# Four raw weight tiles, ten heads kept on chip and a sum load on another queue in a one-core transformer layer

## The chip, the cores and the metric

One core of a Trainium2 chip runs the whole layer. The metric is device time in microseconds, from launch to end. Most executions of one kernel agree within 0.3%.

## The reference, cut to what matters

DEPTH is 1, so the layer is one forgetting-attention (FoX) block and one squared-ReLU MLP, all in float32, for 512 positions of width 2048, 16 heads of 128 and an inner MLP width of 8192.

```python
h = rmsnorm(x, norm_g[0, 0])
q, k, v, f = split(h @ w_in)                      # 3 x 2048 columns and 16 gates
cum = cumsum(log_sigmoid(f + b_f))
logits = q @ k.T * 128**-0.5 + cum_i - cum_j      # causal, per head
h = concat_heads(softmax(logits) @ v) @ w_out
x = x + rmsnorm(h, norm_g[0, 1])
h = square(relu(rmsnorm(x, norm_g[0, 2]) @ w1)) @ w2
x = x + rmsnorm(h, norm_g[0, 3])
```

## The kernel before, in words

**Split products.** Every float32 operand is cut into a high part (a cast by ScalarE, ACT) and a low part (a subtraction by VectorE, DVE), and each product is three matmuls: high by high, high by low, low by high (`mm3`, lines 94 to 96, and `mm3b`, lines 451 to 453). So a weight block on its way to TensorE (PE) passes three stations: a load issued on the queue of SyncE (SP) into a raw tile, an ACT cast, and a DVE subtraction (`load_split`, lines 87 to 89, and `split7`, lines 429 and 430).

**Sevens.** 30 of the 32 blocks of the MLP (a block is 256 of its 8192 inner columns) use a seven-product scheme in place of eight products: a raw tile gets four loaded quarters (512 KB), DVE makes three sums of them (lines 443 to 445), and the seven slots are split at once (`load_seven`). A raw tile has eight slots, and the split reads slots 1 to 7. Three raw tiles take turns (`spool`, `bufs=3`). The split seven goes to one of three places (`tplaces`); one such weight unit feeds 42 matmuls. The other two blocks of the first product are "plain": `plain(hf, p)` runs eight input blocks for the first half of the positions and again for the second half, and loads and splits its weights both times.

**Order of the work.**
1. Projections and attention, head by head, up to about 655 us. `values` copies the output of head h to a tile (tag `o32`, four buffers) and stores it in DRAM (`od`, line 352). The output projection loads all 16 heads back (`split_o`, lines 390 to 393).
2. The output projection: four column blocks c, each with four PSUM banks `py`, all from the pool `psum_acc`; after each block `evac_y` multiplies and squares them (lines 498, 499). Then residual, norm and transposition (`turn`, in the banks of `psum_att`), then `plain` into the banks `ph` of `psum_acc`.
3. The first MLP product: `evac` of the two plain blocks (relu, square, sums: lines 683, 667, 671 to 674), then 30 blocks n of four weight units g each. The squared results go to DRAM (`hd`).
4. The second MLP product: five chunks of six blocks. A chunk is four column pieces cp, each of six weight units k (8 banks in turn), and its sums are added into DRAM by accumulating stores (`md`, line 805) on the queue of GpSimd (POOL). Its left operand is fetched by `want(n)`: a load of 896 KB on POOL's queue into an `h7` tile (`hpool`, two buffers, line 657) and the same split, into a ring of eight places.
5. In the last chunk `gather(cp - 1)` reads the finished sums of the piece before back (`m`, two loads of 896 KB on SP's queue, line 752) into two tiles of `spool`, after the weight unit k = 3 of piece cp, and DVE combines them (lines 755 to 761). `last_w` loads the weights of the two plain blocks into tiles of `spool` too (lines 726 to 729).
6. The tail: `gather(3)`, the products of the plain blocks (`pz`), the last norm, and the output.

Each engine and each queue runs its instructions in the order of the program. A planner sets that order when the kernel is built, from the order of the code, the readiness of operands and free buffers; an instruction that waits holds up all that stand behind it on the same engine or queue.

Of the kernel before, what the change touches and what calls it, by code (L numbers as in the profile page):

```python
# [15 lines left out]
P = 128  # L16
S = 512
# [15 lines left out]
CHUNK = 6  # L33
WARM = 9
# [5 lines left out]
def fox_layer(ctx, tc, xT, x, wq, wk, wv, wf, wo, w1p, w1s, w2s, w2p, gcol, grow, bf, out):  # L40
# [124 lines left out]
    with ExitStack() as att:  # L165
# [106 lines left out]
        ap_ = att.enter_context(tc.tile_pool(name="ap_", bufs=1))  # L272
        def proj(h):
# [25 lines left out]
        def attention(h, res, vs, v32):  # L299
# [44 lines left out]
            def values():  # L344
# [4 lines left out]
                nc.tensor.matmul(ps[:, (TT - 1) * P:], v32[:, c], pts[TT - 1], start=False, stop=True)  # L349
                o = ap_.tile([P, S], F32, tag="o32", name=f"o32_{h}", bufs=4)  # L350
# [72 lines left out]

    AOF = [1, 6, 0, 4, 3, 5, 2]

# [9 lines left out]

    def load_seven(src, name):
# [10 lines left out]
        return split7(raw[:, 1:8], tplaces[tplace[0] % len(tplaces)])  # L447
# [28 lines left out]
    with ExitStack() as trs:  # L476
# [47 lines left out]
        def turn(hf, p):  # L524

            ps = psum_att(f"xT_{hf}_{p}")
# [52 lines left out]
        py = [psum_acc(f"py_{NC - 1}_{t}") for t in range(TT)]  # L579
# [20 lines left out]
        ph = [psum_acc(f"ph_{f}") for f in range(4)]  # L600

        def plain(hf, p):
            w = load_split(w1p[p], f"a{hf}_{p}")
            cols = slice(256 * hf, 256 * (hf + 1))
            for kh in range(2):
# [5 lines left out]
                for f in range(4):  # L611
                    a = [zz[:, kh * 512 + f * P:kh * 512 + (f + 1) * P] for zz in w]
                    mm3(ph[f][:, cols], a, b, p == 0 and kh == 0, p == 7 and kh == 1)
# [12 lines left out]
        for p in range(3):  # L626
            x4[p] = turn(1, p)
            if p < 2:
                m4[p] = mix(p, x4[p])
        for p in range(8):  # L630
            plain(1, p)
            split_mix(p, m4[p])
            if p + 2 < 8:
                m4[p + 2] = mix(p + 2, x4[p + 2])
            if p + 3 < 8:
                x4[p + 3] = turn(1, p + 3)
# [273 lines left out]
```

## Time and profile before

| | us |
|---|---|
| three runs | 2239.34, 2237.58, 2233.78 |
| median | 2237.58 |
| the profiled execution | 2236.39 |
| its span, first to last instruction | 2234.6 |
| PE busy in the span | 2133.5 (95%) |
| DVE, ACT, POOL busy | 1501.1, 958.5, 258.2 |
| PE's granted clock, mean of the span | 0.983 |

Busy PE time is counted from the start to the modelled end of each matmul, and matmuls overlap, so a full PE row says only that it never had to wait. A granted clock of 1.00 is the level of 2.4 GHz and 0.50 that of 1.2 GHz; a mean between them tells how much of a stretch was at each.

### The profile page before, as it was taken

Reading aid. Unit: us, or ns where it says so; the run is one execution under the profiler, and the core shown is the slowest. Engines: PE = TensorE matmul, PEld = TensorE weight load, DVE = VectorE, ACT = ScalarE, POOL = GpSimd, SP = SyncE. Lnnn points to the kernel's source line nnn. Section 1 sums busy time; section 2 is a strip of 40 time slices with the busy share of each in tenths; the row PEclk is TensorE's granted clock in tenths of the full one; section 3 lists DMA queues with packets and bytes.
Section 4 is the critical chain, followed back from the end, with each engine's and each line's share of the span. In section 5 each row is a group of like instructions: output and inputs, shape, how many; then the busy total and the mean of one; then the engine's idle time right before and its main releaser. Section 6 shows DMA issues by size and latency. Waiting matters only on the chain.

```text
span 2234.6 us, 34858 instructions
## 1 busy us (share of the span) xinstructions
PE 2133.5 (95%) x14450; PEld 1979.9 (89%) x14450; DVE 1501.1 (67%) x2007; ACT 958.5 (43%) x1141; POOL 258.2 (12%) x342
## 2 busy tenths in 40 slices
PE   8999999999989998999999999999999999999785
PEld 6788888888867878999999999999999999998774
DVE  9553453544542368888888888888777767676656
ACT  4433332333332356444444444445554545453341
POOL 8000000000010000000000000001122122211113
PEclk9999999999999999999999999999999999999998
DMA  5333333333352364544445444456586878677567
GB/s 176 105 104 94 101 98 99 100 94 104 91 192 89 118 228 145 194 161 163 159 144 166 163 159 143 162 189 231 182 239 164 241 171 239 169 200 187 148 180 225
DMA packets 112351, 352.94 MB, mean 158 GB/s; under 512 B 12080, under 2 KB 23472, under 8 KB 107712
## 3 DMA queue, kind: packets, MB, share of 16 engines
q1 hardware_dynamic: 82656, 246.58, 34.3%
q0 software_dynamic: 29392, 104.12, 17.5%
q8 instruction: 113, 1.85, 0.3%
q14 instruction: 46, 0.38, 0.0%
q10 hardware_dynamic: 144, 0.02, 0.0%
HBM read 268.85 MB, written 81.82 MB: 157 GB/s over the span
## 4 chain that ended last, share of the span: by engine, by line
PE 64%; issue 20%; DVE 7%; POOL 4%; DMA 3%; ACT 1%; SPq 0%; POOLq 0%; DVEq 0%; ACTq 0%
PE ps L453 9%; PE ps L452 9%; PE ps L451 9%; POOL md L805 4%; PE pq L96 3%; PE pk L96 3%; PE pk L94 3%; PE pq L95 3%; PE pk L95 3%; PE pq L94 3%; PE py L94 2%; PE py L95 2%; PE py L96 2%; PE pv L95 2%; PE pv L96 2%
## 5 line engine op out<-in xcount | busy, mean ns | idle before, releaser
L452 PE MATMUL po<-opr 128*128 128x256 f32 x1204 | 343.7, 287 | 24.0 <-DVE opr L430 24.0
L451 PE MATMUL po<-opr 128*128 128x256 f32 x1204 | 337.7, 285 | 6.5 <-ACT opr L429 4.3
L453 PE MATMUL po<-opr 128*128 128x256 f32 x1204 | 341.9, 285 | 0.0
L451 PE MATMUL ps<-opr 128*128 128x256 f32 x1120 | 318.2, 284 | 6.6 <-ACT opr L429 6.6
L452 PE MATMUL ps<-opr 128*128 128x256 f32 x1120 | 318.0, 284 | 0.0
L453 PE MATMUL ps<-opr 128*128 128x256 f32 x1120 | 317.4, 284 | 0.2 <-DVE opr L430 0.2
L452 PEld LDWEIGHTS po<-opr 128*128 128x128 f32 x1204 | 234.0, 194 | 26.9 <-DVE opr L430 26.7
L451 PEld LDWEIGHTS po<-opr 128*128 128x128 f32 x1204 | 230.9, 194 | 8.4 <-ACT opr L429 5.7
L453 PEld LDWEIGHTS po<-opr 128*128 128x128 f32 x1204 | 233.9, 194 | 0.0
L451 PEld LDWEIGHTS ps<-opr 128*128 128x128 f32 x1120 | 216.2, 193 | 6.8 <-ACT opr L429 6.8
L452 PEld LDWEIGHTS ps<-opr 128*128 128x128 f32 x1120 | 216.1, 193 | 0.0
L453 PEld LDWEIGHTS ps<-opr 128*128 128x128 f32 x1120 | 215.7, 193 | 0.5 <-DVE opr L430 0.5
L429 ACT CAST opr<-seven_b 128x1792 fp32r<-128x1792 f32 x86 | 145.2, 1689 | 144.2 <-DVE seven_b L445 68.6
L430 DVE TENSOR_TENSOR opr<-seven_a,opr 128x1792 fp32r<-128x1792 f32 x80 | 161.9, 2024 | 51.5 <-ACT opr L429 50.2
L429 ACT CAST opr<-seven_a 128x1792 fp32r<-128x1792 f32 x80 | 134.7, 1684 | 142.4 <-PE ps L452 131.4
L430 DVE TENSOR_TENSOR opr<-seven_b,opr 128x1792 fp32r<-128x1792 f32 x86 | 173.5, 2020 | 18.5 <-ACT opr L429 18.5
L443 DVE TENSOR_TENSOR seven_b<-seven_b 128x512 f32<-128x512 f32 x120 | 82.7, 689 | 125.7 <-DMA seven_b<-in_w2s 124.9
L451 PE MATMUL ps<-opr,w 128*128 128x256 f32 x560 | 158.5, 283 | 0.0
L452 PE MATMUL ps<-opr,w 128*128 128x256 f32 x560 | 158.5, 283 | 0.0
L453 PE MATMUL ps<-opr,w 128*128 128x256 f32 x560 | 158.5, 283 | 0.0
L452 PE MATMUL po<-w,opr 128*128 128x256 f32 x476 | 136.8, 288 | 9.4 <-DVE w L430 9.4
L805 POOL DMA_DIRECT2D md<-st x112 | 100.2, 1483 | 355.2 <-ACT st L801 354.4
(231 smaller groups left out, 5275.7 us busy)
## 6 DMA issues: line engine op xcount, KB each, us to landing
seven_a<-in_w1s SPq DMA_DIRECT2D x120, 512.0 KB, 3.6
seven_b<-in_w2s SPq DMA_DIRECT2D x120, 512.0 KB, 4.6
md<-st POOLq DMA_DIRECT2D x140, 256.0 KB, 8.1
hd<-ev POOLq DMA_DIRECT2D x30, 1024.0 KB, 4.4
h<-hd POOLq DMA_DIRECT2D x30, 896.0 KB, 5.6
raw_o<-in_wo SPq DMA_DIRECT2D x40, 512.0 KB, 3.5
raw_q<-in_wq SPq DMA_DIRECT2D x32, 512.0 KB, 3.7
raw_k<-in_wk SPq DMA_DIRECT2D x32, 512.0 KB, 3.7
```

Source lines behind the costliest of these rows:

```text
L94: nc.tensor.matmul(o, a[0], b[0], start=start, stop=False)
L95: nc.tensor.matmul(o, a[0], b[1], start=False, stop=False)
L96: nc.tensor.matmul(o, a[1], b[0], start=False, stop=stop)
L429: nc.scalar.copy(hi, z)
L430: nc.vector.tensor_tensor(out=lo, in0=z, in1=f32(hi), op=ALU.subtract)
L443: nc.vector.tensor_tensor(out=raw[:, 4:6], in0=raw[:, 1:3], in1=raw[:, 0:1].to_broadcast([P, 2, 256]), op=ALU.add)
L451: nc.tensor.matmul(o, a[0], b[0], start=start, stop=False, skip_group_check=True)
L452: nc.tensor.matmul(o, a[0], b[1], start=False, stop=False, skip_group_check=True)
L453: nc.tensor.matmul(o, a[1], b[0], start=False, stop=stop, skip_group_check=True)
L805: nc.gpsimd.dma_start(md[cp, :, j], st, accum_op=ALU.add)
```

## The change

- `spool` has four raw tiles of seven slots; the third and fourth sum overwrite slot 0 and fill slot 6, and `BOF` tells the matmuls where each of the seven now is. `hpool` has one `h7` tile in place of two.
- `gather` loads `m` on POOL's queue, after k = 5 in place of k = 3.
- The outputs of heads 0 to 9 stay in tiles of their own; heads 10 to 15 go through DRAM as before.
- The second half of the plain blocks runs in the order 5, 6, 7, 4, 0, 1, 2, 3 and uses the split weights of 5, 6 and 7 that the first half left; the first seven block (n = 2) takes its units in the order 3, 2, 0, 1, and the evacuation of the two plain blocks comes after the second and third of them.
- Column blocks of the output projection alternate between the two PSUM pools, and `ph`, `turn` and the banks of the first product swap pools to fit.

```diff
@@ values / split_o
+                if h < KEEP:
+                    o32[h] = ap_.tile([P, S], F32, tag=f"o32_{h}", name=f"o32_{h}")
+                    nc.scalar.copy(o32[h], ps)
+                    return
...
-            o = ap_.tile([P, S], F32, tag="o32", name=f"o_{h}", bufs=4)
-            nc.sync.dma_start(o, od[h])
+            o = o32.get(h)
+            if o is None:
+                o = ap_.tile([P, S], F32, tag="o32", name=f"o_{h}", bufs=4)
+                nc.sync.dma_start(o, od[h])
@@ load_seven
-        raw = spool.tile([P, 8, 256], F32, tag="seven", name=f"seven_{name}")
+        raw = seven(f"seven_{name}")
         nc.sync.dma_start(raw[:, 0:4], src)
...
-        nc.vector.tensor_tensor(out=raw[:, 6], in0=raw[:, 4], in1=raw[:, 2], op=ALU.add)
-        nc.vector.tensor_tensor(out=raw[:, 7], in0=raw[:, 3], in1=raw[:, 6], op=ALU.add)
+        nc.vector.tensor_tensor(out=raw[:, 0], in0=raw[:, 4], in1=raw[:, 2], op=ALU.add)
+        nc.vector.tensor_tensor(out=raw[:, 6], in0=raw[:, 3], in1=raw[:, 0], op=ALU.add)
@@ turn, output projection, plain
-            ps = psum_att(f"xT_{hf}_{p}")
+            ps = psum_acc(f"xT_{hf}_{p}")
...
-            py = [psum_acc(f"py_{c}_{t}") for t in range(TT)]
+            py = [(psum_att if c % 2 else psum_acc)(f"py_{c}_{t}") for t in range(TT)]
...
-        ph = [psum_acc(f"ph_{f}") for f in range(4)]
+        ph = [psum_att(f"ph_{f}") for f in range(4)]
...
-            w = load_split(w1p[p], f"a{hf}_{p}")
+            order = LATE if hf else range(8)
+            if hf == 0 or p < 5:
+                w[p] = load_split(w1p[p], f"a{hf}_{p}")
@@ pools
-    spool = second.enter_context(tc.tile_pool(name="spool", bufs=3, reuse_waits="tile"))
+    spool = second.enter_context(tc.tile_pool(name="spool", bufs=4, reuse_waits="tile"))
...
-    hpool = hs_.enter_context(tc.tile_pool(name="hpool", bufs=2, reuse_waits="tile", side="right"))
+    hpool = hs_.enter_context(tc.tile_pool(name="hpool", bufs=1, reuse_waits="tile", side="right"))
@@ first MLP product
-        for n in range(2):
+        def evac_plain(n):
...
+            order = [3, 2, 0, 1] if n == 2 else range(4)
+            for g in order:
...
+                if n == 2 and g in order[1:3]:
+                    evac_plain(order.index(g) - 1)
@@ gather
-            nc.sync.dma_start(m, md[cp, :, :, t * 256:(t + 1) * 256])
+            nc.gpsimd.dma_start(m, md[cp, :, :, t * 256:(t + 1) * 256])
...
-                        if cp > 0 and k == 3:
+                        if cp > 0 and k == 5:
```

## Rows read from the trace of the kernel before

**Rows 1.** Page: busy time of PE, and its share of 40 equal slices in tenths.
```profile
PE 2133.5 (95%) x14450; PEld 1979.9 (89%) x14450; DVE 1501.1 (67%) x2007; ACT 958.5 (43%) x1141; POOL 258.2 (12%) x342
...
PE   8999999999989998999999999999999999999785
```

**Rows 2.** Busy time by stretch: length, PE, PEld, DVE, ACT, POOL, clock, DMA, GB/s.
```profile
655.00:682.97 27.97, 18.01 (x72) 14.04 (x71) 8.58 (x12) 6.88 (x11) 0.71 (x2) 0.88 0.47 151
...
865.00:897.20 32.20, 19.99 (x160) 19.00 (x159) 29.76 (x48) 19.50 (x30) 0.55 (x1) 0.93 0.27 94
897.20:1503.00 605.80, 605.58 (x5025) 605.28 (x5026) 516.36 (x687) 276.00 (x216) 18.09 (x34) 1.00 0.48 163
1503.00:1538.00 35.00, 30.02 (x242) 29.00 (x242) 31.14 (x32) 20.82 (x16) 3.70 (x7) 1.00 0.76 255
1538.00:1630.00 92.00, 92.00 (x769) 92.00 (x768) 70.22 (x78) 47.72 (x43) 13.38 (x25) 1.00 0.62 203
...
1752.00:1880.00 128.00, 123.47 (x1013) 122.87 (x1012) 93.51 (x103) 64.06 (x59) 28.30 (x35) 0.99 0.77 201
1880.00:2007.00 127.00, 122.27 (x1004) 121.86 (x1004) 92.27 (x102) 63.92 (x58) 27.71 (x34) 0.99 0.77 197
...
2037.10:2078.40 41.30, 34.21 (x263) 33.40 (x262) 23.66 (x38) 14.07 (x14) 6.19 (x7) 0.92 0.67 166
2078.40:2122.10 43.70, 33.46 (x254) 32.78 (x254) 25.30 (x38) 13.66 (x15) 6.21 (x7) 0.88 0.64 157
2122.10:2172.50 50.40, 41.27 (x288) 38.12 (x287) 32.14 (x42) 21.35 (x25) 6.21 (x7) 0.97 0.68 188
```

**Rows 3.** Waits of PE, whole run: who for whom, us in total, times, longest.
```profile
PE py L94 <- ACT opr L392: 8.4, 3, 6.2
PE ps L451 <- ACT opr L429: 6.6, 1, 6.6
PE ph L96 <- DVE opr L89: 5.5, 3, 2.7
...
PE py L94 <- ACT py L499: 3.7, 1, 3.7
```

**Rows 4.** Two short stretches right after PE waits, columns as in rows 2.
```profile
663.74:667.20 3.46, 3.46 (x8) 2.74 (x9) 1.72 (x3) 1.52 (x3) 0.00 (x0) 0.50 0.57 197
...
897.20:902.70 5.50, 5.28 (x23) 4.98 (x24) 5.47 (x6) 4.30 (x7) 0.54 (x1) 0.50 0.72 251
```

**Rows 5.** DVE by line and shape, 865 to 897.2 us: busy, mean ns.
```profile
L89 DVE TENSOR_TENSOR opr<-raw_a,opr 128x1024 fp32r<-128x1024 f32 x5 | 6.1, 1219 | 0.0
```

**Rows 6.** ACT by line and shape, 865 to 905 us.
```profile
L683 ACT ACTIVATE ev<-ph 128x256 f32<-128x256 f32 x8 | 2.4, 387 | 0.7 <-DMA hd<-ev 0.7
L667 ACT ACTIVATE ev<-ev 128x1024 f32<-128x1024 f32 x2 | 2.1, 1056 | 0.1
```

**Rows 7.** Timeline of POOL's queue, 1480 to 1545 us: start, us, what.
```profile
1494.25 0.54 POOL L657 DMA_DIRECT2D h<-hd  x1 [0.56 <-DVE opr L430]
...
1510.65 0.53 POOL L657 DMA_DIRECT2D h<-hd  x1 [5.90 <-DVE opr L430]
```

**Rows 8.** Timeline of ACT, 1488 to 1530 us.
```profile
1515.39 1.69 ACT L429 CAST opr<-h 128x1792 fp32r<-128x1792 f32 x1 [3.55 <-DMA h<-hd]
```

**Rows 9.** Page: costliest groups, the two halves of a seven's split.
```profile
L429 ACT CAST opr<-seven_b 128x1792 fp32r<-128x1792 f32 x86 | 145.2, 1689 | 144.2 <-DVE seven_b L445 68.6
...
L430 DVE TENSOR_TENSOR opr<-seven_b,opr 128x1792 fp32r<-128x1792 f32 x86 | 173.5, 2020 | 18.5 <-ACT opr L429 18.5
```

**Rows 10.** Page: DMA issues, count, KB each, median us to landing.
```profile
h<-hd POOLq DMA_DIRECT2D x30, 896.0 KB, 5.6
```

**Rows 11.** Timeline of DVE, 1757 to 1764 us.
```profile
1759.89 0.69 DVE L443 TENSOR_TENSOR seven_b<-seven_b 128x512 f32<-128x512 f32 x1 [2.27 <-DMA seven_b<-in_w2s]
```

**Rows 12.** Waits of SP's queue, 2037 to 2176 us.
```profile
SPq L752 <- DMA md<-st: 29.4, 3, 13.9
```

**Rows 13.** DMA view, 2037 to 2078.4 us, 40 equal slices.
```profile
GB/s 0 111 334 194 168 204 178 218 186 204 198 198 95 8 0 28 224 331 371 304 351 172 0 103 317 158 214 281 146 245 71 0 0 0 8 162 340 139 289 75
```

**Rows 14.** Timeline of DVE in the tail.
```profile
2194.73 1.39 DVE L755 TENSOR_TENSOR m<-m 128x256 f32<-128x256 f32 x1 [9.75 <-DMA m<-md]
```

More of the change, by code (lines that the diff above doesn't have):

```diff
@@ L33 @@
 CHUNK = 6
+KEEP = 10
 WARM = 9
@@ L424, in fox_layer @@
     AOF = [1, 6, 0, 4, 3, 5, 2]
+    BOF = [1, 2, 3, 4, 5, 0, 6]
     def split7(z, parts):
@@ L578, in fox_layer @@
         load_g1(NC - 1)
-        py = [psum_acc(f"py_{NC - 1}_{t}") for t in range(TT)]
+        py = [psum_att(f"py_{NC - 1}_{t}") for t in range(TT)]
         for hf in range(2):
@@ L611, in plain @@
                 for f in range(4):
-                    a = [zz[:, kh * 512 + f * P:kh * 512 + (f + 1) * P] for zz in w]
-                    mm3(ph[f][:, cols], a, b, p == 0 and kh == 0, p == 7 and kh == 1)
+                    a = [zz[:, kh * 512 + f * P:kh * 512 + (f + 1) * P] for zz in w[p]]
+                    mm3(ph[f][:, cols], a, b, p == order[0] and kh == 0, p == order[-1] and kh == 1)
         for p in range(8):
@@ L625, in fox_layer @@
         x4, m4 = {}, {}
[L626 to L636, printed above, removed]
+        for i in range(3):
+            x4[i] = turn(1, LATE[i])
+            if i < 2:
+                m4[i] = mix(LATE[i], x4[i])
+        for i in range(8):
+            plain(1, LATE[i])
+            split_mix(LATE[i], m4[i])
+            if i + 2 < 8:
+                m4[i + 2] = mix(LATE[i + 2], x4[i + 2])
+            if i + 3 < 8:
+                x4[i + 3] = turn(1, LATE[i + 3])
     first.close()
     second = ctx.enter_context(ExitStack())
-    spool = second.enter_context(tc.tile_pool(name="spool", bufs=3, reuse_waits="tile"))
+    spool = second.enter_context(tc.tile_pool(name="spool", bufs=4, reuse_waits="tile"))
     hs_ = ctx.enter_context(ExitStack())
     wthird = hs_.enter_context(tc.tile_pool(name="wthird", bufs=1, reuse_waits="tile", side="right"))
-    hpool = hs_.enter_context(tc.tile_pool(name="hpool", bufs=2, reuse_waits="tile", side="right"))
+    hpool = hs_.enter_context(tc.tile_pool(name="hpool", bufs=1, reuse_waits="tile", side="right"))
     w3 = wthird.tile([P, 2 * SLOT + 24], F32R, name="w3")
@@ L704, in fox_layer @@
         for n in range(2, NPAIR):
-            b = [(psum_acc if n % 2 else psum_att)(f"ps_{n}_{i}") for i in range(4)]
-            for g in range(4):
+            b = [(psum_att if n % 2 else psum_acc)(f"ps_{n}_{i}") for i in range(4)]
+            order = [3, 2, 0, 1] if n == 2 else range(4)
+            for g in order:
                 w = load_seven(w1s[n - 2, g], f"a{n}_{g}")
@@ L710, in fox_layer @@
                     for kk in range(2):
-                        p = 2 * g + kk
-                        mm3b(b[bi][:, part * 256:(part + 1) * 256], [zz[:, j, kk * P:(kk + 1) * P] for zz in w], xop(p, AOF[j]),
-                             p == 0 and FIRST[bi] == j, p == 7)
+                        mm3b(b[bi][:, part * 256:(part + 1) * 256], [zz[:, BOF[j], kk * P:(kk + 1) * P] for zz in w], xop(2 * g + kk, AOF[j]),
+                             g == order[0] and kk == 0 and FIRST[bi] == j, g == order[-1] and kk == 1)
+                if n == 2 and g in order[1:3]:
+                    evac_plain(order.index(g) - 1)
                 if n == NPAIR - 1 and g > 0:
@@ L719, in fox_layer @@
     NCHUNK = NSTR // CHUNK
-    bank[0] = 4
+    bank[0] = 0
     wlast, hlast = {}, {}
     def last_w(i):
-        raw = spool.tile([P, 8, 256], F32, tag="seven", name=f"raw_z{i}").rearrange("p n c -> p (n c)")[:, 0:1024]
+        raw = seven(f"raw_z{i}").rearrange("p n c -> p (n c)")[:, 0:1024]
         nc.sync.dma_start(raw, w2p[i // 2, i % 2])
```

11 lines of the change are left out of this document (8 added, 3 removed).

## The prediction

> **What bounds the kernel now.** I read the page first: PE is busy for 2133.5 of 2234.6 us, and its slices are full except near two fifths of the span, and in the last three [rows 1]. So nothing that other engines do in the full slices can help; only the holes can. The second view is the busy time by stretch. From 897.2 to 1503 us PE lacks 0.2 us: the first MLP product cannot gain. Between 1538 and 1630 us PE never waits either, and there 769 matmuls take 92.00 us, 0.1196 us each; a weight unit of 42 is 5.02 us and a piece of six units 30.1 us. Those are the yardsticks. Against them stand the holes: 10.0 us idle from 655 to 682.97, 12.2 from 865 to 897.2, 5.0 from 1503 to 1538, 4.5 and 4.7 in two middle chunks, and the pieces cp = 1, 2, 3 of the last chunk, which take 41.3, 43.7 and 50.4 us where 30.1 would do [rows 2]. Of cp = 3, 36 of the 288 matmuls are 512 wide pz products (288 less 6 x 42); at twice 0.1196 us they explain 8.6 us, so the three pieces lose 11.2 + 13.6 + 11.7 = 36.5 us. The third view, PE's waits, names who is late in the first two holes [rows 3]. A clock cost comes on top: just after such waits the granted clock stands at 0.50, the 1.2 GHz level, after PE had idled [rows 4], and work done there takes double. The waits of SP's queue and the DMA view tell what the last chunk stands for: in three gathers SP waits 29.4 us for the accumulating stores to land before it can issue the load of m [rows 12], and in that time the DMA engines fall to 0 to 95 GB/s with weight loads queued behind [rows 13].
>
> **The change part by part.** Negative is a gain.
>
> *Ten heads kept.* PE waits 8.4 us in three waits for the split of a reloaded head, the longest 6.2 us [rows 3]. Ten of 16 stores and reloads go; the six left have ten heads' worth of PE work to hide behind, if the planner moves loads 10 to 12 ahead. Head 15 must still be stored and reloaded, and one store on SP's queue may still stand ahead of loads 11 to 14; then the 6.2 us stay. With the half clock after it, 3.46 us of which half is lost [rows 4], the part is worth 8.4 + 1.7 = 10.1 at most and 2.2 at least (the two short waits). I take 9.3, near the upper end, because four tiles are free for loads 10 to 12 long before.
>
> *Banks in turn.* The wait for `py` squares, 3.7 us once [rows 3], goes: block 1 starts in the other pool, whose banks the attention has left. The later switches show no wait in that list, so they give nothing. -3.7. Swapping `ph` and `turn` only keeps the parity; 0, and if a bank is late there the cost is that of this row.
>
> *Plain blocks kept split, other order.* Three loads and splits go, 3 x 1.22 us of DVE [rows 5], in a stretch where DVE is busy 29.8 of 32.2 us and PE waits 5.5 us for just this split [rows 2, 3]. That takes off 3.7 and leaves about 1.8. Then the hole of 6.6 us before the first seven: ahead of its ACT split stand four relus and a square, 4 x 0.39 + 1.06 = 2.6 us [rows 6], and DVE's share behind them. With the evacuation moved two units later, what remains is the split itself, 1.69 us of ACT [rows 9] and a handover, say 2.2; so 4.4 go. Units 3 and 2 first need blocks 6, 7, 4 and 5 alone, which are mixed first, so the rest of the mixing is covered by 10 us of PE. The half clock from 897.2 to 902.7 cost 2.7 us [rows 4]; I let half of it go, as a shorter hole remains. 3.7 + 4.4 + 1.4 = 9.5; bounds 4 and 14.9 (5.5 + 6.6 + 2.8, all of it). -9.5. Moving the evacuation costs PE nothing while DVE has its spare sixth (516.4 of 605.8 us busy [rows 2]); if that cover fails, it is the 2.6 us again.
>
> *Four raw tiles.* In the middle chunks the PE waits come from a late weight load, as at 1759.89, where DVE itself waits 2.27 us for it [rows 11]: with three tiles the next load is issued only when a split frees one. A fourth puts each load one unit, 5.02 us, earlier, over twice that wait. I count the idle 4.5 + 4.7 us of both chunks as gone: -9.2; bounds 0 and 12 (with the clock at 0.99). The sum in slot 0 in place of slot 6 costs the same DVE work: 0.
>
> *One h7 tile.* This pays for the fourth raw tile, and is the one cost. At the start of the second product six splits of h are wanted one unit apart. With one tile each load waits for the split before: issue to ACT start 4.74 us (1510.65 to 1515.39 [rows 7, 8]), 1.69 of ACT, 2.02 of DVE [rows 9], 0.3 to the next issue: 8.75 us a turn. Now the second is already in its tile at the start. Then its load cannot go before 1494.25 [rows 7], and the sixth is split at 1494.25 + 5 x 8.75 = 1538. PE starts unit 5 at 1538 - 5.02 = 1533 in the trace: 5 us late. With the median landing of 5.6 us [rows 10] and 1 us of queueing at DVE, a turn is 10.6 and the lateness 14. I take +8, as some of the 5 us that PE waits there now [rows 2] falls together with it. At the later chunk starts four turns of 9 us fit the seven to eight units that the ring gives them: 0, bound +8 each (a rival).
>
> *Gather on POOL's queue, two units later.* SP never waits for the stores; weights flow on. POOL has nothing else in the last chunk once the two last h loads are in, so its wait holds nobody until the next stores of sums, a unit later. At k = 5 the stores have had 25 us; the longest wait was 13.9 us [rows 12], so m is there when DVE comes. Two of four tiles are held for some ten us, leaving two for weights. Not all 36.5 us return: the DMA share in these pieces was 0.67, 0.64 and 0.68 of 41.3, 43.7 and 50.4 us [rows 2], 27.7, 28.0 and 34.3 us of transfers, against 30.1 + 30.1 + 38.7 us of PE. cp = 1 and 2 would run the engines over 90% full. I take 32 + 33 + 43.4 = 108.4 in place of 135.4: -27; bounds 12 (only SP's part of cp = 1 and 2) and 36.5. *Against it speaks a rule.* The Trainium skill (DMA: Bandwidth & Descriptors, "Issuing engines are not separate DMA queues") says that DMAs of all queues share the same 16 engines, and that issuing from several saves only the sequencer's time to start them. By that rule alone this part would be near nothing and the time that of the second rival; the idle slices in rows 13 show that here the engines stood without work, which the rule does not speak of.
>
> *The tail.* DVE waits 9.75 us for m, until 2194.73 [rows 14]; the load still waits for the same stores. The reload of x now goes ahead of it and may take bandwidth from the stores: 0, bounds -4 and +8.
>
> **The sum.** 2234.6 - 9.3 - 3.7 - 9.5 - 9.2 + 8 - 27 = 2183.9 us of span. The profiled execution lies 1.8 us above its span (2236.39), and 1.2 us below the median of the runs shown: 2183.9 + 1.8 + 1.2 = 2186.9, so 2187.
>
> **The rivals.**
> 1. *The single h7 tile bites at all five chunk starts.* For it: its split is in order on ACT and DVE, so a late h load holds the weight splits behind it. Against: four turns have 35 us there. 8 us at four more starts, and the middle gain gone: 2187 + 32 + 9 = 2228 at worst, 2214 with two thirds of it.
> 2. *The last chunk stays bound by transfers.* For it: engines over 90% full, eight weight loads more in cp = 3. Only the issue of six loads is saved, some 0.54 us each as POOL's loads take [rows 7]: 3.2 in place of 27: 2211. (The rule of the skill named above gives this.)
> 3. *Slower: POOL's queue stands.* Where an h load waits up to 9 us for its only tile, stores of sums stand behind it, their staging tiles fill, ACT stops at the next copy and with it every split. It decides from 51 us, the whole net gain: six such stops. Twenty pieces offer places, but PE works ahead by two units, 10 us, and covers most: 2245.
> 4. *Everything returns.* No cost at the second product (its present 5 us gone too), all clock losses back: 13.8 + 14.9 + 5 + 12 + 36.5 = 82.2 us: 2155.
> 5. *The reload stall stays,* as the head-15 store stands ahead: 2187 + 7.1 = 2194; inside the range.
>
> **How the numbers follow.** Forecast with its neighbour 5: 0.62, by itself 2172 to 2202. Rival 1: 0.12, rival 2: 0.13, rival 3: 0.06, rival 4: 0.07. The range goes from 2160, which takes in part of rival 4, to 2219, with rival 2 and most of rival 1; outside are 0.04 below and 0.06 + 0.05 above. Faster or slower counts from 0.3%, 6.7 us, which is about what a measurement of this kernel tells from no change. All but rival 3 and the far end of rival 1 are faster: 0.90; same 0.04, slower 0.06.
>
> **What would show it.** In the profile after: no PE wait for L392 and for the squares of py beyond 2 us; a hole of about 2 us at the first seven; SP's queue without a wait for md; pieces of 32 to 33 us in the last chunk and some 43 for the last; a longer stretch for the first piece of the second product, with PE waiting for the split of h. I am wrong if PE waits for splits of h at every chunk, if the last pieces still take over 40 us, or if ACT's copies of po wait for stores through POOL.

## The result and the profile after

The changed kernel takes 2213.11 us (median; 2210.34 to 2215.27) against 2235.68 us for the kernel before: ratio 0.990, 95% interval 0.988 to 0.992. That is faster, by 22.6 us and not by the 50 that I forecast; it lies inside the range. The profiled execution has a span of 2210.4 us, 24.2 less than before. Lines moved: `mm3` is now L95 to L97, `split7` L440 and L441, the seven's sums L457 to L459, `mm3b` L465 to L467, the evacuation L702, L686 and L690 to L692, the load of m L773.

The page: busy time of PE and its 40 slices. The slices answer to [rows 1]: both early holes stay, a new dip stands at the start of the second product (slice 28, 1492 to 1547 us), and the last three are shallower in sum.

```profile
PE 2130.7 (96%) x14450; PEld 1979.9 (90%) x14450; DVE 1498.8 (68%) x2004; ACT 953.0 (43%) x1138; POOL 267.9 (12%) x350
...
PE   8999999999989998999999999998999999999896
```

Busy time by stretch, columns as in [rows 2]: the end of the plain blocks, the first piece of the second product, its three middle chunks, and the four pieces of the last chunk.

```profile
855.00:887.00 32.00, 20.85 (x166) 19.85 (x165) 29.57 (x46) 19.12 (x29) 0.55 (x1) 0.93 0.32 115
...
1494.00:1535.60 41.60, 34.17 (x249) 32.95 (x248) 34.49 (x39) 18.50 (x12) 3.19 (x6) 0.92 0.60 194
1626.60:1749.50 122.90, 121.43 (x1010) 121.03 (x1009) 93.89 (x103) 63.41 (x60) 25.69 (x34) 1.00 0.75 208
1749.50:1875.60 126.10, 123.27 (x1022) 122.46 (x1020) 93.81 (x103) 63.39 (x60) 28.11 (x34) 1.00 0.78 203
1875.60:2003.20 127.60, 122.09 (x996) 120.98 (x995) 93.83 (x103) 63.54 (x60) 28.22 (x34) 0.99 0.77 201
2003.20:2035.90 32.70, 29.86 (x233) 29.26 (x232) 24.74 (x28) 15.17 (x16) 7.87 (x10) 0.95 0.77 201
2035.90:2069.70 33.80, 31.93 (x264) 31.52 (x264) 23.04 (x36) 14.05 (x14) 8.20 (x9) 1.00 0.74 193
2069.70:2107.40 37.70, 32.87 (x255) 32.46 (x253) 24.74 (x38) 13.53 (x14) 8.19 (x9) 0.91 0.72 181
2107.40:2148.10 40.70, 36.37 (x275) 34.77 (x274) 27.34 (x33) 19.01 (x20) 8.18 (x9) 0.96 0.82 229
```

Set against the kernel before by the start of the first instruction of each stage (a piece is counted from its first copy of sums to the next piece's), the span divides so:

| stage | before | after | difference | forecast |
|---|---|---|---|---|
| start to the first `py` product | 622.7 | 618.2 | -4.6 | 0 |
| output projection, to the first `ph` | 207.8 | 202.5 | -5.3 | -13.0 (heads, banks) |
| plain blocks, to the first seven | 66.7 | 66.0 | -0.7 | -9.5 |
| first product | 607.7 | 607.9 | +0.2 | 0 |
| second product, first chunk | 126.0 | 132.0 | +6.0 | +8 |
| its three middle chunks | 378.1 | 376.4 | -1.7 | -9.2 |
| last chunk | 163.4 | 145.0 | -18.4 | -27 |
| from the last piece's copies to the end | 62.1 | 62.3 | +0.2 | 0 |

The first two rows have to be read together. Of the first difference, 1.0 us is the load prologue; the rest is the mark itself, which moved. Before the change, eleven matmuls of the last head's scores (`s`) and a wait of 0.99 us stand ahead of the first `py` product; after it, those eleven run behind the first 24 of `py`. PE of the kernel before, from the first of them to the first `py`:

```profile
619.24 0.39 PE L313 MATMUL s<-k,q 128*128 128x128 f32 x2
...
622.73 0.50 PE L94 MATMUL py<-opr 128*128 128x512 f32 x1 [0.99 <-ACT opr L392]
```

So from the start to the first `ph` product the change gained 9.8 us, 8.9 without the prologue, where heads and banks were to give 13.0. The last chunk holds 12 `pz` products in place of 36, yet the tail that takes up the other 24 is no longer for them: m of the last gather ends it either way.

Waits of PE over the whole run, columns as in [rows 3]. The wait for the squares of `py`, 3.7 us, is gone. The hole before the first seven is still 6.6 us, the reloads still cost 6.5.

```profile
PE po L466 <- DVE opr L441: 18.4, 14, 4.6
PE po L465 <- ACT opr L440: 7.2, 5, 2.7
PE ps L465 <- ACT opr L440: 6.6, 1, 6.6
PE py L95 <- ACT opr L401: 6.5, 2, 5.3
PE ph L97 <- DVE opr L90: 4.5, 4, 1.6
```

### The profile page after: what moved, and what is told of

Read it like the earlier page. It is cut to its first block, busy times and chain, and to the rows that moved or that the text cites. A ratio compares the mean times of both kernels' runs of the same rounds, so it can differ in the third digit from the quotient of the medians.

```text
span 2210.4 us, 34770 instructions
## 1 busy us (share of the span) xinstructions
PE 2130.7 (96%) x14450; PEld 1979.9 (90%) x14450; DVE 1498.8 (68%) x2004; ACT 953.0 (43%) x1138; POOL 267.9 (12%) x350
## 3 DMA queue, kind: packets, MB, share of 16 engines
q1 hardware_dynamic: 72048, 232.42, 32.7%
## 5 line engine op out<-in xcount | busy, mean ns | idle before, releaser
L466 PE MATMUL po<-opr 128*128 128x256 f32 x1204 | 344.7, 287 | 18.5 <-DVE opr L441 18.4
L465 PE MATMUL po<-opr 128*128 128x256 f32 x1204 | 341.1, 286 | 6.2 <-ACT opr L440 6.0
L467 PE MATMUL po<-opr 128*128 128x256 f32 x1204 | 340.4, 285 | 1.1 <-DVE opr L441 1.1
L465 PE MATMUL ps<-opr 128*128 128x256 f32 x1120 | 318.3, 284 | 6.6 <-ACT opr L440 6.6
L467 PE MATMUL ps<-opr 128*128 128x256 f32 x1120 | 317.5, 284 | 0.2 <-DVE opr L441 0.2
L465 PEld LDWEIGHTS po<-opr 128*128 128x128 f32 x1204 | 232.4, 194 | 7.8 <-ACT opr L440 7.0
L467 PEld LDWEIGHTS po<-opr 128*128 128x128 f32 x1204 | 232.6, 194 | 1.5 <-DVE opr L441 1.3
L465 PEld LDWEIGHTS ps<-opr 128*128 128x128 f32 x1120 | 216.2, 193 | 6.8 <-ACT opr L440 6.8
L467 PEld LDWEIGHTS ps<-opr 128*128 128x128 f32 x1120 | 215.8, 193 | 0.5 <-DVE opr L441 0.5
L441 DVE TENSOR_TENSOR opr<-seven_a,opr 128x1792 fp32r<-128x1792 f32 x80 | 161.9, 2024 | 51.5 <-ACT opr L440 50.2
L440 ACT CAST opr<-seven_b 128x1792 fp32r<-128x1792 f32 x86 | 145.1, 1693 | 115.5 <-PE po L467 88.2
L440 ACT CAST opr<-seven_a 128x1792 fp32r<-128x1792 f32 x80 | 134.8, 1685 | 139.0 <-PE ps L466 133.4
L441 DVE TENSOR_TENSOR opr<-seven_b,opr 128x1792 fp32r<-128x1792 f32 x86 | 173.7, 2020 | 19.8 <-ACT opr L440 19.6
L457 DVE TENSOR_TENSOR seven_b<-seven_b 128x512 f32<-128x512 f32 x120 | 82.6, 688 | 125.5 <-DMA seven_b<-in_w2s 125.1
L465 PE MATMUL ps<-opr,w 128*128 128x256 f32 x560 | 158.5, 283 | 0.0
L467 PE MATMUL ps<-opr,w 128*128 128x256 f32 x560 | 158.5, 283 | 0.0
L465 PE MATMUL po<-w,opr 128*128 128x256 f32 x476 | 136.3, 286 | 3.5 <-ACT w L440 2.3
L466 PE MATMUL po<-w,opr 128*128 128x256 f32 x476 | 136.2, 286 | 1.8 <-DVE w L441 1.8
```

Source lines behind the costliest of these rows:

```text
L440: nc.scalar.copy(hi, z)
L441: nc.vector.tensor_tensor(out=lo, in0=z, in1=f32(hi), op=ALU.subtract)
L465: nc.tensor.matmul(o, a[0], b[0], start=start, stop=False, skip_group_check=True)
L466: nc.tensor.matmul(o, a[0], b[1], start=False, stop=False, skip_group_check=True)
L467: nc.tensor.matmul(o, a[1], b[0], start=False, stop=stop, skip_group_check=True)
```

## The experiments

An effect is read from the stage that an edit touches. Ratios are to the kernel before, run beside each; its medians there lay between 2235.5 and 2239.9 us, 4.4 apart, so medians decide only what is larger. All edits are to the changed kernel unless the text says the kernel before.

### The reloaded heads

SP's queue in the changed kernel, timeline from 645 us: start, us, what. The store of head 15 (`od`, L359) waits for that head, and the reloads behind it (L399) are issued only at 651.4 and later. Rival 5 of the prediction.

```profile
645.99 0.43 SPq L399 DMA_DIRECT2D o<-od  x1
651.07 0.33 SPq L359 DMA_DIRECT2D od<-o  x1
651.44 0.94 SPq L399 DMA_DIRECT2D o<-od  x2
652.48 0.40 SPq L88 DMA_DIRECT2D raw_o<-in_wo  x1
654.87 1.10 SPq L399 DMA_DIRECT2D o<-od  x2
```

**e1**, other ten heads:

```diff
-                if h < KEEP:
+                if h >= H - KEEP:
```

> The last ten heads are kept on chip instead of the first ten, so no head that goes through DRAM is stored late. Theory (the store of head 15 stands on SP's queue ahead of the reloads of heads 11 to 14, as the trace of the changed kernel shows): the waits of PE for the split of a reloaded head, 1.19 and 5.33 us, fall to 1.5 us together at most and the half clock that follows them (657.3, 6.8 us) goes with them; the span falls by 5 to 9 us, to 2201 to 2205. Rival (the reloads are late because SP's queue is full of weight loads, or because DMA is busy there): a wait of 4 us or more for a split of a head stays and the span is within 3 us of 2210.

2204.98 us, ratio 0.986 (0.984 to 0.988), span 2201.8. PE has no wait for L401 left, nor the half clock near 657; from the first `py` product to the first `ph` 192.3 us in place of 202.5, -10.2. The theory holds: the number of heads kept was right, the choice of heads was not. From the start to the first `ph` that makes 19.0 us against the kernel before, without the prologue, more than the 13.8 that the prediction allowed for heads and banks together: 12.1 are their waits, and most of the rest goes with the half clock, which stood for 17.0 us of this part before (at 660.5, 684.3 and 814.1) and for 3.4 here, where the prediction took 1.7.

### The hole before the first seven

ACT in the changed kernel, timeline: the evacuation (L702, L686) stands before the first split (L440) as it did before the change, though the code has it later. But ACT then idles 3 us for DVE's last sum (L459), ahead of which DVE ran its own share of the evacuation (L690 to L692, 1.5 us): the relus on ACT were not what came last.

```profile
879.68 1.20 ACT L702 ACTIVATE ev<-ph 128x256 f32<-128x256 f32 x4
880.92 1.06 ACT L686 ACTIVATE ev<-ev 128x1024 f32<-128x1024 f32 x1
884.96 1.69 ACT L440 CAST opr<-seven_a 128x1792 fp32r<-128x1792 f32 x1 [2.99 <-DVE seven_a L459]
```

**e4**, the order forced:

```diff
+        split[0] = nc.scalar.copy(hi, z)                  # in split7
+        split[1] = nc.vector.tensor_tensor(out=lo, ...)
...
-                    evac_plain(order.index(g) - 1)
+                    with tc.issue_after(split[0].ins), tc.issue_after(split[1].ins):
+                        evac_plain(order.index(g) - 1)
```

> The evacuation of the two plain pairs is forced behind the split of the seven that stands ahead of it in the code, on ACT and on DVE; nothing else is changed. Theory (the hole of 6.62 us before the first seven is the relus and the square on ACT, and DVE's share of the evacuation, which were issued ahead of the first split although the code has them later): the hole falls to 2 to 3 us and the span by 4 to 7 us, to 2203 to 2206. Rival (DVE's backlog of mixing sets the start): the hole stays above 5 us and the span within 2 us of 2210, or the work moved behind the split makes PE wait at the second or third seven by as much.

2212.54 us, ratio 0.990 (0.988 to 0.992), span 2206.1. The hole falls from 6.62 to 4.29 us and no further, so neither expectation is met whole; the stage gains 2.3, which the medians cannot tell. ACT and DVE of this run show what is left: the split still waits, now 2.9 us, and DVE reaches the sums (L458) only when the last mixed block is split (L579), which ran behind the half of the mixing that ACT holds.

```profile
882.09 1.69 ACT L440 CAST opr<-seven_a 128x1792 fp32r<-128x1792 f32 x1 [2.86 <-DVE seven_a L460]
```

```profile
879.27 1.22 DVE L579 TENSOR_TENSOR opr<-m,opr 128x1024 fp32r<-128x1024 f32 x1 [1.28 <-ACT opr L578]
880.41 0.68 DVE L458 TENSOR_TENSOR seven_a<-seven_a 128x512 f32<-128x512 f32 x1
```

Sums ahead of the mixing were not tried.

### The last chunk: queue, place or tiles

**e3**, the other queue at the new place; **f1**, the old place with the new queue; **f2**, the kernel before with the new place alone:

```diff
-            nc.gpsimd.dma_start(m, md[cp, ...])           # e3
+            nc.sync.dma_start(m, md[cp, ...])
...
-                        if cp > 0 and k == 5:             # f1; f2 is the reverse, in the kernel before
+                        if cp > 0 and k == 3:
```

> The loads of m are back on SP's queue, at the same place (two units later than in the kernel before). Theory (SP stood for the stores): the last chunk grows from 145 us to 153 or more, as SP again waits some 10 us in each of three gathers, two units later than before; span 2218 to 2226. Rival (the last chunk is bound by raw tiles held by m, or by transfers, whatever queue issues the load, as the Trainium skill's rule in DMA: Bandwidth & Descriptors, Issuing engines are not separate DMA queues, would have it): the last chunk stays within 3 us of 145 and the span within 3 us of 2210; then the two units of delay made the gain, not the queue.

> The changed kernel with the gather put back two units earlier (after the fourth unit of a piece in place of the sixth); the loads of m stay on POOL's queue. With the loads on SP's queue at the later place the last chunk took 141.2 us, with POOL's 145.0. Theory (the later place made the gain, the queue none): with the early place the last chunk grows to 152 us or more although POOL issues the loads, since the tiles of m, two of the four raw tiles, are held until the stores have landed; span 2216 to 2224. Rival (either POOL's queue or the later place is enough by itself): the last chunk stays within 3 us of 145.

> The kernel before the change with one part alone: the gather two units later, its loads still on SP's queue, three raw tiles of eight slots. Theory (place alone): the last chunk falls from 163.4 us to 150 or less, the span from 2234.6 to 2221 or less, and SP's waits for the accumulating stores fall from 29.4 us to under 10. Rival (the place helps only together with seven-slot tiles or kept heads): the last chunk stays above 158 us.

**g3**, a tile of its own for m, in the memory of the fourth raw tile:

```diff
-    spool = ... bufs=4
+    spool = ... bufs=3
...
-                            gather(cp - 1, ep, seven)
+                            gather(cp - 1, ep, lambda name: mp.tile([P, 7, 256], F32, tag="m", name=name))
```

> The changed kernel with three raw tiles, one h7 tile, and a tile of its own for m in the last chunk, in the memory of the fourth raw tile; m on POOL's queue at the later place. With three raw tiles shared with m the last chunk took 152.9 us and the span 2221.4; with four shared, 145.0 and 2210.4. Theory (what the last chunk still loses is raw tiles that m holds): it falls to 146 or less. Rival (it is DVE's work for the gathers, or the transfers): it stays within 3 us of 152.9.

| kernel | queue, place, raw tiles | last chunk | DVE's waits for m in it | median, ratio (95%) |
|---|---|---|---|---|
| before | SP, k = 3, three | 163.4 | 18.9 | |
| f1 | POOL, k = 3, four | 168.8 | 21.5 | 2233.77, 0.999 (0.998 to 1.000) |
| f2 | SP, k = 5, three | 146.8 | 3.9 | 2220.41, 0.993 (0.991 to 0.995) |
| after | POOL, k = 5, four | 145.0 | 5.2 | 2213.11, 0.990 |
| e3 | SP, k = 5, four | 141.2 | 1.7 | 2210.25, 0.989 (0.987 to 0.991) |
| g3 | POOL, k = 5, three and one for m | 171.8 | 30.0 | 2240.75, 1.001 (0.9995 to 1.003) |

The place makes the gain in this chunk: alone, in the kernel before, it gives 17.5 us of span (f2, as its theory said), and put back it takes the whole gain of the change away (f1, by 8 us more than its theory allowed). At the later place POOL's queue gives nothing: e3's theory fell, its chunk is the shorter one. At the early place that queue was run with four raw tiles only, and did not help there. With SP's queue at the later place SP waits for the stores (`md<-st`) 7.0 us in two waits where it waited 29.4 in three [rows 12]. SP's waits in the last chunk: first the changed kernel, then e3, the largest each and the one for m or its stores. With POOL's queue SP stands all the same, for raw tiles that DVE has yet to free (L441; before the change this wait was 45.0 us, for L430), and 20.8 us behind loads of m, where it was 8.4.

```profile
SPq L456 <- DVE opr L441: 37.5, 8, 9.6
SPq L456 <- DMA m<-md: 20.8, 2, 10.4
```

```profile
SPq L456 <- DVE opr L441: 37.6, 8, 9.9
...
SPq L773 <- DMA md<-st: 7.0, 2, 3.8
```

SP's wait for the stores was not the price: f1 has none, and its chunk is no shorter than before the change. The prediction had read [rows 13] too quickly. While SP stood in the first gather, from 2037.6 to 2051.84, the DMA engines of the kernel before were under 100 GB/s in 8 of 40 equal slices only, 2.8 us of 14.2:

```profile
GB/s 0 81 81 150 196 368 403 282 138 161 167 167 196 190 201 190 196 184 178 201 201 247 173 190 190 224 196 184 196 201 213 196 196 167 109 35 17 12 0 0
```

What the traces show at the early place is DVE's standing, which the prediction did not price (raw tiles that m keeps for longer are a second price, see h3; no run takes the two apart at that place). DVE in f1: it arrives at the first sum of m (L776) and stands 8.29 us, with the weights' splits behind it; of the 30.1 us of a piece's six units it needs 6 x 3.55 = 21.3 for the weights (0.69 + 0.42 + 0.42 + 2.02 each) and 14 x 0.42 = 5.9 for the gather, so it has about 3 us to spare.

```profile
2046.08 2.02 DVE L441 TENSOR_TENSOR opr<-seven_b,opr 128x1792 fp32r<-128x1792 f32 x1 [1.59 <-ACT opr L440]
2056.39 0.43 DVE L776 TENSOR_TENSOR m<-m 128x256 f32<-128x256 f32 x1 [8.29 <-DMA m<-md]
...
2059.73 2.02 DVE L441 TENSOR_TENSOR opr<-seven_b,opr 128x1792 fp32r<-128x1792 f32 x1
```

The theory for g3 (raw tiles that m holds) was not met, and against both expectations the chunk grew by 19 us over the 152.9 of the same three tiles shared (f3, below): with a single tile for m the second load can start only when DVE has used the first, and DVE stands for both, 30.0 us in six waits against 5.4 us in f3.

**h3**, in the kernel g2 below, takes the other side: DVE never stands for m, as its arithmetic is forced behind the split of the unit in which m is loaded.

```diff
+            with (tc.issue_after(split[1].ins) if cp < 3 else ExitStack()):
                 nc.vector.tensor_tensor(out=p6, in0=p1, in1=p6, op=ALU.add)
...
```

> The best combined kernel with the arithmetic of the three gathers inside the last chunk forced behind DVE's split of the unit in which m is loaded, so that DVE does not stand for m with the weights' sums behind it. Theory (DVE's standing is what the gathers cost): pieces 2 to 4 of the last chunk, 35.4, 36.1 and 39.2 us, fall by 4 us or more in sum. Rival (the tiles that m holds are the cost): m is held longer and the pieces grow by 2 us or more in sum.

2203.08 us, ratio 0.985 (0.982 to 0.987), against 2189.1 for g2. DVE has no wait for m, but m holds its two raw tiles longer, 10.7 to 18.7 us from the issue of a load to its last use in place of 7.3 to 9.3; pieces 2 to 4 take 34.1, 40.9 and 49.8 us, 14.1 more in sum (1.7 of it seven more `pz` products inside). The rival holds here. So both cost: DVE that stands, and tiles that m holds. In these runs the gather is cheap where m lands just before DVE comes.

### The memory trade

**e2** undoes it, **f3** takes the fourth raw tile alone away:

```diff
-    spool = ... bufs=4
+    spool = ... bufs=3                                    # e2 and f3
...
-    hpool = ... bufs=1
+    hpool = ... bufs=2                                    # e2
```

> The memory trade alone is undone: three raw tiles (of seven slots) and two h7 tiles. Theory A (a fourth raw tile gains nothing in the middle chunks, and the single h7 tile costs only at the start): the first chunk of the second product falls from 132 to 126 us, the middle chunks stay within 1 us of 122.8, 126.0 and 127.6, the last chunk grows from 145 to 150 or more since m takes two of three tiles; span 2207 to 2215. Theory B (the fourth tile does gain some 9 us in the middle chunks and the single h7 tile takes them back): the middle chunks change by 3 us or more in sum against those of the kernel before the change. What tells them apart is the idle time of PE in the three middle chunks.

> The changed kernel with three raw tiles and the single h7 tile: the fourth raw tile alone is taken away. With four and one the middle chunks took 122.8, 126.0 and 127.6 us and the last 145.0; with three and two 123.9, 127.4, 125.6 and 150.0, 4 us of that being pz products that run inside. Theory (the fourth raw tile gains nothing in the middle chunks): they stay within 2 us of 376.4 us in sum. Rival (the fourth tile gains about what the single h7 tile costs there): their sum grows by 5 us or more, and the last chunk to 150 or more.

| kernel | raw, h7 | first chunk | middle three | last | median |
|---|---|---|---|---|---|
| after | 4, 1 | 132.0 | 376.4 | 145.0 | 2213.11 |
| e2 | 3, 2 | 125.1 | 377.2 | 150.0 | 2212.83 |
| f3 | 3, 1 | 134.2 | 375.5 | 152.9 | 2221.78 |

e2 has the ratio 0.990 (0.988 to 0.992), f3 0.994 (0.992 to 0.995). The trade is worth nothing. In the first chunk the single h7 tile costs 9.1 us (f3 against e2), of which the fourth raw tile gives 2.2 back. With the single h7 tile the fourth raw tile is worth 8.7 us of the median and 11.0 of the span (f3): besides those 2.2 it gives 7.9 in the last chunk, 4.5 of it 19 `pz` products that with three tiles run inside, and 3 behind it. In the middle chunks, where I had looked for 9.2, it gives nothing: without it they are no longer. Single middle chunks moved by up to 1.9 us in e2, beyond the 1 of its theory A, their sum by less than 1; f3 met its theory there. Where expectations below give 376.9 for e2 and 369.6 for f4 (the next section), the lengths in the traces are 377.2 and 369.9.

### The order of the splits of h

Three of the six PE waits over 0.9 us in the middle chunks of the changed kernel (1778, 1892 and 1904, 4.5 of 9.3 us) come within 5 us of a split of h on DVE. The other three (1700, 1825, 1953) lie 25 us or more from any, otherwise than the expectation of f4 has it; ACT's seventh copy of a piece had waited 2.0 to 4.8 us for a store some 6 to 11 us before them. ACT in the changed kernel ahead of PE's wait at 1778: it stands 8.65 us for h, with weight splits behind it.

```profile
1771.52 1.70 ACT L440 CAST opr<-h 128x1792 fp32r<-128x1792 f32 x1 [8.65 <-DMA h<-hd]
1773.13 3.27 ACT L440 CAST opr<-seven_b 128x1792 fp32r<-128x1792 f32 x2
```

**f4** forces that split behind the next weight split; **h1** does the same with three raw tiles and two h7, and **i2** in the kernel before with nothing else changed:

```diff
+        if 3 <= n < NSTR - 2:                             # f4: if n >= 3
+            h_late.append((n, h7))
+            return
...
                     w = load_seven(w2s[n, cp], f"b{n}_{cp}")
+                    while h_late:
+                        with tc.issue_after(split[0].ins), tc.issue_after(split[1].ins):
+                            h_ready(*h_late.pop())
```

> The changed kernel with the splits of h from the fourth on forced behind the split of the next seven of weights on ACT and on DVE. In the changed kernel every PE wait over 0.9 us in the middle chunks comes within a few units of such a split (1700, 1778, 1825, 1892, 1904 and 1953 us). Theory (the split of h stands ahead of the weights' split on ACT and DVE, and waits there for its load): the idle time of PE in the three middle chunks, 9.3 us in waits over 0.9 us, falls below 5; the start of the second product (132.0 us) may get worse, as its splits come later still. Rival (DVE and ACT lack time at these places whatever the order): the waits move and keep their sum within 2 us.

> The changed kernel with the memory trade undone (three raw tiles, two h7 tiles) and the splits of h forced behind the next seven of weights, as in the run where that took the middle chunks from 376.4 to 369.6 us with four raw tiles and one h7 tile. Theory (the gain needs the fourth raw tile: loads that are a unit earlier): the middle chunks stay within 2 us of the 376.9 us that three and two gave without the forced order. Rival (the order alone makes the gain, and the fourth tile none): they fall to 371 us or less.

> The kernel before the change with nothing changed but the splits of h from the fourth to the twenty-eighth, forced behind the next seven of weights. The prediction put the PE waits of its middle chunks (378.1 us for the three, PE idle 10.5 us) down to a late weight load that only a further raw tile could mend. Theory now (order): the three chunks fall to 370 us or less with the three raw tiles that it has, and the span by 7 to 11 us. Rival (the prediction's reading): they stay above 375 us.

f4: 2209.81 us (0.988; 0.987 to 0.990), middle chunks 369.9 and PE's waits over 0.9 us in them 4.3, as the theory had it, but the last 150.9, where the last two h now come late. h1: 2200.65 (0.984; 0.982 to 0.986), middle chunks 366.7 with three raw tiles and two h7, better than f4's four and one. i2: 2226.78 (0.996; 0.994 to 0.998), middle chunks 364.9 in place of 378.1, span 8.8 less, both as the theory had it. Busy time of i2 by stretch, its middle chunks: PE does not wait at all.

```profile
1628.30:1749.30 121.00, 121.00 (x1011) 121.00 (x1010) 94.27 (x102) 64.06 (x60) 25.60 (x34) 1.00 0.77 210
1749.30:1870.30 121.00, 121.00 (x1010) 121.00 (x1010) 93.95 (x102) 64.19 (x60) 28.11 (x34) 1.00 0.82 212
1870.30:1993.20 122.90, 122.90 (x1026) 122.90 (x1026) 95.74 (x104) 65.68 (x61) 28.64 (x35) 1.00 0.80 212
```

The order alone makes the gain; the prediction's reading of [rows 11] fell, on the kernel that it was read from. DVE of the kernel before, ahead of those rows: splits of h (L430 `h`, 2.02 us each, four from 1739.82 to 1757) each take a turn ahead of a weight split. A raw tile is freed by that weight split, so the next load is issued late, and what the trace then names is the load: the one that DVE waits for at 1759.89 [rows 11] was issued at 1753.54, when the split from 1751.49 had ended (the SP row).

```profile
1744.75 2.02 DVE L430 TENSOR_TENSOR opr<-h,opr 128x1792 fp32r<-128x1792 f32 x1
1746.68 2.02 DVE L430 TENSOR_TENSOR opr<-seven_b,opr 128x1792 fp32r<-128x1792 f32 x1
...
1749.56 2.02 DVE L430 TENSOR_TENSOR opr<-h,opr 128x1792 fp32r<-128x1792 f32 x1
1751.49 2.02 DVE L430 TENSOR_TENSOR opr<-seven_b,opr 128x1792 fp32r<-128x1792 f32 x1
...
1755.26 2.02 DVE L430 TENSOR_TENSOR opr<-h,opr 128x1792 fp32r<-128x1792 f32 x1
```

```profile
1753.54 0.33 SPq L442 DMA_DIRECT2D seven_b<-in_w2s  x1
```

The forced order changes more than the turn. ACT's waits for h in the three middle chunks, first in the kernel before, then in i2:

```profile
ACT opr L429 <- DMA h<-hd: 22.7, 9, 3.9
```

```profile
ACT opr L429 <- DMA h<-hd: 5.3, 1, 5.3
```

The splits of h also stand farther apart (on DVE at 1732, 1742, 1753 and 1764 us, before at 1732, 1740, 1745, 1750, 1755 and 1765), and a weight load lands in 4.1 us at the median in place of 4.7. So the order is shown as the cause, but not how much of it is the turn on DVE, ACT's standing for h, or loads that no longer come in a bunch.

Not all of i2's gain reaches the end: its last chunk is 170.6, 7.2 more. Its first piece is 4 us longer (32.2 against 28.1), probably as the splits no longer run ahead; that, and the rest, stays open.

### Together

**g1** is e1, e3, e4 and f4 (but not for the last two h) in one; **g4** the same with m on POOL's queue; **g2** is g1 with the second h in a raw tile; **h2** is g2 with the two last plain h in raw tiles too; **i1** is g1 with three raw tiles and two h7.

```diff
-        h7 = h_tile(f"h7_{n}")
+        h7 = seven(f"h7_{n}") if n == 1 else h_tile(f"h7_{n}")          # g2, h2
...
-        raw = h_tile(f"hz_{i}").rearrange(...)
+        raw = seven(f"hz_{i}").rearrange(...)                           # h2
```

> The changed kernel with four corrections, each tried alone before: the last ten heads kept (-8.4 us of span), the evacuation of the plain pairs forced behind the first splits (-4.3), the splits of h from the fourth to the twenty-eighth forced behind the next seven of weights (middle chunks -6.8, first -2.2), the loads of m on SP's queue at the later place (0 to -3.8). If they add, as they lie in different stages: 2210.4 - 8.4 - 4.3 - 6.8 - 2.2 - 1.9 = 2186.8 us of span, 2189 by the clock of the runs; each that overlaps with another leaves the span above 2195.

> The same four corrections but the loads of m on POOL's queue, as in the changed kernel: the queue alone is compared, at the later place and with nothing else late. Theory (by then the stores have landed, so no queue stands): within 3 us of the same kernel with SP's queue. Rival (POOL's queue hurts, since m holds raw tiles before its load can start): 4 us slower, all of it in the last chunk.

> The combined kernel (m on SP's queue), and the second h of the second product loaded into one of the four raw tiles, so that two h are on chip at the start as in the kernel before. Theory (the first chunk's 130 to 132 us against 125 with two h7 tiles is the second h that has no tile): the first chunk falls to 126 us or less and the span by 4 to 6. Rival (the raw tile that it takes holds back the first weights): the first chunk stays above 128.

> The best combined kernel (second h in a raw tile) with the two last plain h, too, loaded into raw tiles in place of the single h7 tile. In its trace four loads of h follow one another through that one tile at the start of the last chunk, and the first piece there takes 36.3 us where 30.2 would do. Theory (that chain): the first piece falls to 33 us or less and the span by 3 or more. Rival (the wait of ACT's seventh copy for the stores, 4.2 us at 2020, or raw tiles taken from the weights): it stays above 35.

> The changed kernel with the memory trade undone (three raw tiles, two h7 tiles) and the four corrections: last ten heads kept, evacuation forced behind the first splits, splits of h forced behind the weights', m on SP's queue. If the gains add to the 2197.2 us of span that three and two with the forced order of h gave: 2197.2 - 8.4 - 4.3 = 2184.5, and 0 to 2 less from SP's queue. Rival (four tiles are worth something once everything else is in order): 2190 or more, slower than the four-tile kernel with the second h in a raw tile (2187.3).

| kernel | first chunk | middle three | last | span | median | ratio (95%) |
|---|---|---|---|---|---|---|
| g1 | 129.8 | 373.3 | 148.4 | 2199.2 | 2203.05 | 0.985 (0.982 to 0.987) |
| g4 | 131.3 | 370.7 | 150.7 | 2202.8 | 2204.04 | 0.985 (0.983 to 0.987) |
| g2 | 121.0 | 370.7 | 147.0 | 2187.3 | 2189.1 | 0.980 (0.977 to 0.982) |
| h2 | 120.2 | 369.5 | 148.2 | 2184.2 | 2186.33 | 0.978 (0.976 to 0.981) |
| i1 | 123.2 | 365.7 | 148.1 | 2182.4 | 2186.54 | 0.979 (0.977 to 0.980) |

g1 did not add up: 11.2 of the 23.6 us, since the hole gave 2.3 as in e4's own trace, the middle chunks half of what f4 had, and the last chunk and what follows it took back 3.4 and 2.5. g4 tells no queue from the other: 1.0 us in the medians, 3.6 in the spans. g2 met its theory and more, 8.8 us in the first chunk. h2 shortened the first piece of the last chunk from 36.3 to 31.7 as its theory said, and the other three gave that back (+5.8); it is not told from g2. i1, with as many raw and h7 tiles as before the change, is as fast as any; its gains added up (2182.4 us of span, 2184.5 expected), and its rival fell: four raw tiles buy nothing that three and two with the same order, place and heads do not. Its page:

```profile
PE 2122.4 (97%) x14450; PEld 1972.4 (90%) x14450; DVE 1501.9 (69%) x2004; ACT 955.8 (44%) x1138; POOL 259.3 (12%) x342
...
PE   8999999999999998999999999999999999999986
```

## Why the prediction was wrong

- **Ten heads kept** (-9.3): the wait fell only from 8.4 to 6.5 us, and 6.8 us of half clock stayed behind it. The failed step is "six left have ten heads' worth of PE work to hide behind"; the store of head 15 stands ahead of the reloads, as the text itself feared. With other heads kept the stretch gave 10.2 more (e1). So the size of this part was if anything too small, as it priced the half clock too low.
- **Banks** (-3.7): right; the wait is gone and none took its place, and the half clock behind it (3.4 us at 684.3) is gone with it.
- **Plain blocks** (-9.5): the failed step is "with the evacuation moved two units later, what remains is the split itself". It was not moved: the planner kept it ahead. Nor was it the price: forced, it gave 2.3 of the 4.4 (e4); what is left comes from DVE's mixing and sums, not from ACT's relus. The three splits saved 1.0 us of PE's waits (5.5 to 4.5), not 3.7. The 1.4 for the half clock did not come either: 10.2 us at 0.50 from 892.6 before, 10.2 from 882.6 after.
- **Four raw tiles** (-9.2): the mechanism was wrong, and the failed step is "A fourth puts each load one unit, 5.02 us, earlier". A late load was taken for a lack of tiles; it was the order of the splits on ACT and DVE, which free them. The middle chunks changed by -1.7 with the whole change, and the tile gave nothing in them (e2, f3); the order, 13.2 in the kernel before (i2).
- **One h7 tile** (+8): right in place and near in size: +6.0, 6.9 for the trade (e2), and 9.1 for the tile by itself (f3 against e2). Rival 1, the same at every chunk start, came at the last chunk alone: its first piece takes 32.2 to 34.6 us in the runs with one h7 tile and the planner's order of the splits, 27.9 to 28.2 in those with two. That is half of what the last chunk fell short by.
- **Gather** (-27): place and size of the loss were right, its split between queue and place not. The failed step is "SP waits 29.4 us for the accumulating stores to land [...] and in that time the DMA engines fall to 0 to 95 GB/s": in the wait that [rows 13] show they were under 100 GB/s for a fifth of the time, and without any such wait of SP the chunk was no shorter (f1). That "weights flow on" failed too: SP stands for raw tiles as before, and longer behind m. What cost was DVE's standing for m, 18.9 us before and 5.2 after. The later place alone gave 16.6 in this chunk, and POOL's queue nothing at that place (f2, e3, g4); the three pieces took 112.2 us where 108.4 were forecast, though 24 `pz` products (5.7 us) had left them, and the first piece, for which no change was forecast, grew from 28.1 to 32.7 (see the single h7 tile). The rule that the prediction weighed (the Trainium skill, DMA: Bandwidth & Descriptors, "Issuing engines are not separate DMA queues") speaks of the queue alone, and in these runs the queue was indeed worth nothing (2210.25 and 2213.11 us, 2203.05 and 2204.04). Rival 2's 2211 came near the time by luck: the last chunk did shorten, and other parts fell short.
- **The tail** (0): right.

The sum of the misses: heads and banks 4.1, plain blocks 8.8, middle chunks 7.5, last chunk 8.6, less 1.0 in the prologue and 2.0 in the first chunk, and 0.4 elsewhere: 26.4 of the 26.5 us of span by which the forecast was off (2183.9 against 2210.4).

Still open: what holds the last chunk at 145 to 148 us where four pieces at 30.1 us and 12 `pz` products (2.9 us) would take 123. Standing for m and held tiles each make it longer, but no run freed it of both. In g2 ACT's seventh copy of a piece waits 4.16 us for an accumulating store, as there are six staging tiles, and two splits stand behind it; a seventh tile was not tried.

```profile
2020.42 0.59 ACT L835 COPY st<-po 128x512 f32<-128x512 f32 x1 [4.16 <-DMA md<-st]
2020.90 3.27 ACT L440 CAST opr<-seven_b 128x1792 fp32r<-128x1792 f32 x2
```

## What to carry to other kernels

When an engine waits for a load, look at what freed the load's buffer before you buy another buffer: here splits that came too early, on ACT and DVE, held it, and order alone gave more than the tile. A read of data that is still being stored was made cheap here by asking later, not by asking on another queue; then look who stands for its arrival and what its buffer withholds. A step that is moved in the code is moved only when the built order shows it.

## What the runs showed that I had not expected

A weight load of 512 KB, 4.3 us at the median, took 7.3 us in the changed kernel when it was issued at 2072.57 among seven accumulating stores, and PE then waited 4.6 us at 2082.61, the longest wait of its second product. 24 `pz` products, 5.7 us of PE at twice 0.1196 us each, moved into the tail and left its length as it was, 62.1 and 62.3 us.
